# Experts of a two-layer MoE trunk in a fixed order, with the branch for overflowing rows ahead of them and a quarter of the value products moved

## The chip, the core and the metric

The kernel runs on one core of a Trainium2 chip. The core has a matrix engine (PE, with its weight loads shown apart as PEld), a vector engine (DVE), a scalar engine (ACT), GpSimd (POOL) and SyncE (SP), which here issues the DMAs that bring in the weights. The time is the device time of one execution in microseconds; of the kernel before there are three: 1061.95, 1063.36 and 1065.77, median 1063.36.

## What is computed

Two layers over 512 rows of 1024 values, all in float32. A layer has a token mixer beside a cross-attention to 256 fixed memory rows, an output projection and a layer norm, then a mixture of experts and another layer norm. This work concerns the mixture:

```
scores = sigmoid(x @ router_w);  a group of 4 experts of 16 is chosen, and 2 experts in it
gate   = their two scores, normalised;  combine[t, e] = gate of expert e for row t, else 0
for e in range(16):
    h   = silu(x @ w_gate[e]) * (x @ w_up[e])          # 1024 -> 512
    out = out + combine[:, e:e+1] * (h @ w_down[e])    # 512 -> 1024
```

The cross-attention of layer 1 needs `k, v = split(mem @ w_kv)`, which doesn't depend on the rows; the kernel computes it while layer 0's routing runs.

## The kernel before, in words

**Products.** A float32 product is three products of parts: each weight tile is copied to a high part on ACT (L168) and the rest, raw minus high, is made on DVE or GpSimd (L169); `mm3` (L202 to L204) multiplies high by high, low by high and high by low. Right-hand sides are split in the same way (`split_to`, L207 on ACT and L208 on DVE).

**Weights.** A class `Stream` (W) brings all weights in order, 1 MB a load, by SP (L147), into raw pages of 8 KB a partition. There are 24 pages, which the mixture's other tiles share too. `W.rings(8)` sets eight of them aside for split parts (ten after expert 5, which leaves nine for raw weights in layer 0 and eleven in layer 1). `flight` is how many loads may be under way (four in the mixture), `keep` how many pages stay free (four from expert 12 on). `W.pump()` issues splits and loads as long as there are pages, and is called at the end of each `W.done(g)`, when a split tile has been used. `W.on_pool(n)` says which splits go to GpSimd.

**An expert.** `gather(e)` (L667) fetches up to 128 rows by an indirect DMA of GpSimd; `xtrans(e)` transposes them (L676) and splits them to `xgt`; `gate_up(e)` makes 48 products into `ga` and `ua`, Silu on ACT (L692) and the multiplication on DVE (L693); `htrans(e)` transposes h (L699) and splits it to `ht`; `down(e)` makes 24 products into `ya` and two evictions on ACT with the gate as scale (L714); `scatter(e)` (L663) adds the rows to the result by an indirect DMA. The loop issues for each e: gate_up(e), xtrans(e+1), gather(e+3), down(e-1) and its scatter, htrans(e). An expert's weights are six loads: gate, up, gate, up in halves of the 1024 rows, then two of the down weights of the expert before.

**Overflow.** Rows beyond 128 of an expert are left to `more(i, ...)` (L887): every engine reads the number `nover` (L889) and branches (L890) around a loop that the data rarely enter. It is called in the loop at e == 0, and its page `rest` is dropped behind it. An engine that reads the number waits for DVE's last write, and its earlier work has to be done before it.

**Order.** The tile scheduler decides each engine's order by its own simulated times; a `tc.manual_schedule` makes it keep the order of the code on the engines named, and `tc.issue_after(x)` keeps an instruction behind x.

**Layer 0's head.** While the routing runs (tables made by `tab` products, L626), `fill0` calls `keys_values()`: keys (`ka`), then 48 value products (`va`) in four quarters (j), then two splits to `vt`. In it GpSimd takes some of the splits.

Of the kernel before, what the change touches and what calls it, by code (L numbers as in the profile page):

```python
# [23 lines left out]
OP = mybir.AluOpType  # L24
# [3 lines left out]
P = 128  # L28
# [19 lines left out]
def trunk(ctx, tc, x, mem, w_in_a, sgu_ln_g, sgu_ln_b, sgu_w, sgu_b, w_in_b, conv_w, w_kv, w_out,  # L48
# [15 lines left out]
    def page(name, shape, dtype=FT, of=None):  # L64
        of = free_pages if of is None else of
        assert of, f"no page for {name}; held: {sorted(v[1] for v in held.values())}"
        i = of.pop(0)
        uid[0] += 1
        t = pages.tile(shape, dtype, name=f"{name}_{uid[0]}", tag=f"pg{i}", bufs=1)
        held[id(t)] = (i, name, t)  # L70
        return t

    def drop(*ts):
        for t in ts:
            i, name, _ = held.pop(id(t))
            W.home(name).append(i)
# [123 lines left out]
    def mm3(o, a, b, start, stop):  # L200

        pe.matmul(o, a[0], b[0], start=start, stop=False)  # L202
        pe.matmul(o, a[0], b[1], start=False, stop=False)  # L203
        return pe.matmul(o, a[1], b[0], start=False, stop=stop)  # L204
# [111 lines left out]
    drop(memp)  # L316
    keep_warm(8)

    def keys_values():
        kt = page("kt", [P, 2, H, NMEM], FR)  # L320
        vt = page("vt", [P, 2, 2, MW], FR)
        a = [acc("ka") for _ in range(H)]
        for j in range(4):
            g = W.next()
            for kk in range(2):
                k = 2 * j + kk
                for h in range(H):
                    cs = slice(h * P, (h + 1) * P)
                    mm3(a[h][:, :NMEM], (g[:, 0, kk, cs], g[:, 1, kk, cs]), (memh[:, k, :], meml[:, k, :]),
                        k == 0, k == KB - 1)  # L330
            W.done(g)
        for h in range(H):
            split_to(kt[:, 0, h, :], kt[:, 1, h, :], a[h][:, :NMEM])
        a = [acc("va") for _ in range(2)]
        for j in range(4):
            g = W.next()
            for kk in range(2):
                k = 2 * j + kk
                for m in range(2):
                    ms = slice(m * P, (m + 1) * P)  # L340
                    mm3(a[m], (memh[:, k, ms], meml[:, k, ms]), (g[:, 0, kk, :], g[:, 1, kk, :]),
                        k == 0, k == KB - 1)
            W.done(g)
        for m in range(2):
            split_to(vt[:, 0, m, :], vt[:, 1, m, :], a[m])
        return kt, vt
# [303 lines left out]
    def experts(i, lnp, fill, after, stop, fine=False):  # L650
# [15 lines left out]
        def gather(e):  # L666
            pool_e.indirect_dma_start(out=xg[:, e % 2], out_offset=None, in_=x1d[i],  # L667
                                      in_offset=bass.IndirectOffsetOnAxis(ap=tabs[e][0], axis=0),
                                      bounds_check=S - 1, oob_is_err=False)
# [9 lines left out]
        def gate_up(e, between=None):  # L679
            a = [acc("ga"), acc("ua")]  # L680
            for half in range(2):
                if half and between is not None:
                    between()
                for u in range(2):
                    for j in range(2):
                        g = W.next()
                        for kk in range(2):
                            k = 4 * half + 2 * j + kk
                            m = mm3(a[u], (xt[:, 0, k, :], xt[:, 1, k, :]), (g[:, 0, kk, :], g[:, 1, kk, :]),
                                    k == 0, k == KB - 1)  # L690
                        W.done(g)
            act.activation(hp[:, 0, :], a[0], AF.Silu)  # L692
            vec.tensor_tensor(hp[:, 1, :], hp[:, 0, :], a[1], op=OP.mult)  # L693
            return m

        def htrans(e):
# [5 lines left out]
        def down(e, evict):  # L702
            for n in range(2):
                o = acc("ya")
                for j in range(2):
                    g = W.next()
                    for kk in range(2):
                        k = 2 * j + kk
                        mm3(o, (ht[:, 0, k, :], ht[:, 1, k, :]), (g[:, 0, kk, :], g[:, 1, kk, :]), k == 0, k == 3)
                    W.done(g)  # L710
                evict(n, o)

        def scaled(e):
            return lambda n, o: act.activation(ys[e % 2][:, n * 512:(n + 1) * 512], o, AF.Copy, scale=tabs[e][1])  # L714
# [4 lines left out]
            with tc.issue_after(last_entry[-1]):  # L719
                keep_warm(8)  # L720
        fill()
        rest = page("more", [P, 4, FE])
        W.keep, W.flight = 0, 4
        W.ahead, W.whole, W.on_pool = 6, True, lambda n: False
        W.rings(8)
        W.pump()
        xtrans(0)
        gather(2)
        for e in range(E):
            up = gate_up(e, (lambda: (down(last - 1, scaled(last - 1)), scatter(last - 1))) if e == last else None)  # L730
            if e + 1 < E:
                xtrans(e + 1)
            if e + 3 < E:
                gather(e + 3)
            if e == 0:
                more(i, rest)
                drop(rest)
                W.pump()
            if e == 5:
                W.parts += 2  # L740
            if 0 < e < last:
# [326 lines left out]
    W.keep = 3  # L1068

    def fill0():  # L1070
        kv1.append(keys_values())
        drop(memh, meml)
    xhl = []

# [79 lines left out]
```

## Time and profile before

| | |
|---|---|
| runs | 1061.95, 1063.36, 1065.77 us, median 1063.36 |
| profiled execution, its own time | 1063.26 us |
| its span, first to last instruction | 1061.6 us |
| mean granted clock of PE | 0.970 of 2.4 GHz |
| busy: PE, PEld, DVE, ACT, POOL | 991.3, 812.6, 780.7, 628.6, 170.8 us |
| HBM read, written | 262.22, 26.21 MB |

The span is 1.7 us shorter than the execution's own time, and all rows below are on its clock. Layer 0's experts lie at 215 to 535 us, layer 1's at 730 to 1040. Products are pipelined: a row's length is its latency, and two in a row start closer than that, so the pace is read from starts.

### The profile page before, as it was taken

To read this page: it belongs to the slowest core of one execution; us is meant where nothing else is said; L and a number is where in the kernel's file an instruction comes from. 1 tells how busy PE (TensorE), PEld (TensorE's weight loads), DVE (VectorE), ACT (ScalarE), POOL (GpSimd) and SP (SyncE) were. 2 spreads that over 40 slices of the span, in tenths; PEclk is the share of its full clock that TensorE was granted. 3 is DMA by queue.
4 is the path that set the end of the run, shared out by engine and by line. 5 is a ranking of instruction groups with operands and counts; after the bars stand their busy time and mean duration, and the time that the engine had idled before them with its cause. 6 is when DMAs were issued, how large, how long until landed. Compare 5 with 4: busy or idle time off the path is not lost. (4 is left out here: it accounts for less than half of the span.)

```text
span 1061.6 us, 12769 instructions
## 1 busy us (share of the span) xinstructions
PE 991.3 (93%) x4815; PEld 812.6 (77%) x4816; DVE 780.7 (74%) x880; ACT 628.6 (59%) x682; POOL 170.8 (16%) x115
## 2 busy tenths in 40 slices
PE   8999999769999999899899999986699999998995
PEld 6788889658888887678679887875588888886873
DVE  4638667866889976788794656475789999777885
ACT  4526533446788865767653514232688888767762
POOL 0000004311222212101101000212022222221123
PEclk9999999979999999999999999986899999999998
DMA  9713358568999999999690414492499999999934
GB/s 323 274 41 119 120 198 296 181 224 287 361 371 307 396 350 330 319 319 338 175 390 26 159 51 159 148 390 74 172 362 349 371 341 376 354 356 335 333 67 157
DMA packets 102220, 273.31 MB, mean 257 GB/s; under 512 B 10442, under 2 KB 10966, under 8 KB 102152
## 3 DMA queue, kind: packets, MB, share of 16 engines
q1 hardware_dynamic: 89480, 242.84, 62.8%
q0 software_dynamic: 11808, 26.97, 9.1%
q10 hardware_dynamic: 864, 2.62, 0.7%
q8 instruction: 39, 0.64, 0.2%
q14 instruction: 29, 0.24, 0.1%
HBM read 262.22 MB, written 26.21 MB: 272 GB/s over the span
## 5 line engine op out<-in xcount | busy, mean ns | idle before, releaser
L169 DVE TENSOR_TENSOR low<-raw,high 128x2048 fp32r<-128x2048 f32 x189 | 429.8, 2290 | 90.6 <-ACT high L168 87.2
L168 ACT ACTIVATE high<-raw 128x2048 fp32r<-128x2048 f32 x189 | 358.2, 1913 | 44.8 <-PE ga L204 33.4
L168 ACT ACTIVATE split<-raw 128x1024 fp32r<-128x1024 f32 x66 | 68.5, 1058 | 76.5 <-PE za L204 26.0
L203 PE MATMUL ua<-low,xgt 128*128 128x512 f32 x248 | 97.8, 394 | 9.0 <-DVE low L169 9.0
L202 PE MATMUL ya<-high,ht 128*128 128x512 f32 x256 | 103.5, 406 | 1.3 <-ACT high L168 1.3
L203 PE MATMUL ya<-low,ht 128*128 128x512 f32 x256 | 102.3, 400 | 2.1 <-DVE low L169 2.1
L204 PE MATMUL ya<-high,ht 128*128 128x512 f32 x256 | 101.8, 398 | 0.8 <-DVE ht L208 0.7
L203 PE MATMUL ga<-low,xgt 128*128 128x512 f32 x248 | 99.9, 403 | 2.1 <-DVE low L169 1.9
L202 PE MATMUL ga<-high,xgt 128*128 128x512 f32 x248 | 100.4, 405 | 0.0
L204 PE MATMUL ga<-high,xgt 128*128 128x512 f32 x248 | 98.1, 396 | 0.0
L169 DVE TENSOR_TENSOR split<-raw,split 128x1024 fp32r<-128x1024 f32 x57 | 68.7, 1221 | 39.7 <-ACT split L168 38.9
L202 PE MATMUL ua<-high,xgt 128*128 128x512 f32 x248 | 97.4, 393 | 0.1
L204 PE MATMUL ua<-high,xgt 128*128 128x512 f32 x248 | 96.9, 391 | 0.0
L667 POOL DMA_INDIRECT xg<-x1d,idxs x32 | 49.8, 1556 | 267.6 <-PE xt L676 238.3
L169 POOL TENSOR_TENSOR split<-raw,split 128x1024 fp32r<-128x1024 f32 x9 | 21.7, 2406 | 284.8 <-DVE sto L474 148.9
L207 ACT ACTIVATE xgt<-xt 128x512 fp32r<-128x512 f32 x64 | 36.4, 592 | 50.3 <-PE ua L203 26.0
L202 PE MATMUL za<-xh,split 128*128 128x512 f32 x160 | 61.9, 393 | 2.0 <-ACT xh L207 2.0
L203 PEld LDWEIGHTS ua<-low,xgt 128*128 128x128 f32 x248 | 46.6, 188 | 21.0 <-DVE low L169 11.7
L203 PE MATMUL za<-xl,split 128*128 128x512 f32 x160 | 62.5, 391 | 0.0
L204 PE MATMUL za<-xh,split 128*128 128x512 f32 x160 | 61.5, 390 | 0.0
L203 PEld LDWEIGHTS ya<-low,ht 128*128 128x128 f32 x256 | 48.6, 190 | 13.7 <-DVE low L169 3.1
L202 PEld LDWEIGHTS ya<-high,ht 128*128 128x128 f32 x256 | 48.6, 190 | 12.9 <-ACT high L168 1.8
(250 smaller groups left out, 1899.1 us busy)
## 6 DMA issues: line engine op xcount, KB each, us to landing
raw<-in_w_gate_dram SPq DMA_DIRECT2D x64, 1024.0 KB, 8.8
raw<-in_w_up_dram SPq DMA_DIRECT2D x64, 1024.0 KB, 8.3
raw<-in_w_down_dram SPq DMA_DIRECT2D x64, 1024.0 KB, 9.5
raw<-in_w_kv_dram SPq DMA_DIRECT2D x8, 1024.0 KB, 7.0
raw<-in_w_out_dram SPq DMA_DIRECT2D x8, 1024.0 KB, 6.1
raw<-in_w_in_b_dram SPq DMA_DIRECT2D x8, 1024.0 KB, 10.2
raw<-in_w_in_a_dram SPq DMA_DIRECT2D x6, 1024.0 KB, 5.5
x1d<-x POOLq DMA_DIRECT2D x8, 512.0 KB, 5.8
```

The source lines that it names most:

```text
L168: act.activation(high, src, AF.Copy)
L169: (pool_e if self.on_pool(self.count) else vec).tensor_tensor(low, src, high, op=OP.subtract)
L202: pe.matmul(o, a[0], b[0], start=start, stop=False)
L203: pe.matmul(o, a[0], b[1], start=False, stop=False)
L204: return pe.matmul(o, a[1], b[0], start=False, stop=stop)
L207: r = act.activation(hi, src, AF.Copy)
L667: pool_e.indirect_dma_start(out=xg[:, e % 2], out_offset=None, in_=x1d[i], in_offset=bass.IndirectOffsetOnAxis(ap=tabs[e][0], axis=0), bou ...
```

## The change

1. Experts 0 to 14 are issued under `tc.manual_schedule` for PE, ACT and DVE; it is closed at e == 15, so the last expert is left to the scheduler.
2. `more` moves ahead of the loop, behind `fill()` and ahead of xtrans(0); its scratch is the page of h, and the page `rest` is gone. `W.pump()` stands behind xtrans(0) and gather(2).
3. In `gate_up` Silu is issued right behind gate's last product, and the multiplication ahead of the last `W.done`; in `down` the eviction stands ahead of `W.done`, so each is ahead of the splits which that call issues.
4. In layer 0 the value products of j == 3 are issued behind the last product of the tables, and GpSimd takes no split of `fill0`.

```diff
-    def keys_values():
+    def keys_values(after=None):
...
+                    with ExitStack() if after is None or j < 3 else tc.issue_after(after):
+                        mm3(a[m], (memh[:, k, ms], meml[:, k, ms]), (g[:, 0, kk, :], g[:, 1, kk, :]),
+                            k == 0, k == KB - 1)
...
+                        if half and u and j:
+                            vec.tensor_tensor(hp[:, 1, :], hp[:, 0, :], a[1], op=OP.mult)
                         W.done(g)
-            act.activation(hp[:, 0, :], a[0], AF.Silu)
-            vec.tensor_tensor(hp[:, 1, :], hp[:, 0, :], a[1], op=OP.mult)
+                    if half and not u:
+                        act.activation(hp[:, 0, :], a[0], AF.Silu)
...
+                    if j:
+                        evict(n, o)
                     W.done(g)
-                evict(n, o)
...
         fill()
-        rest = page("more", [P, 4, FE])
+        more(i, hy)
         W.keep, W.flight = 0, 4
         W.ahead, W.whole, W.on_pool = 6, True, lambda n: False
         W.rings(8)
-        W.pump()
         xtrans(0)
         gather(2)
+        W.pump()
+        order = ExitStack()
+        order.enter_context(tc.manual_schedule(engines={ET.PE, ET.Activation, ET.DVE}))
         for e in range(E):
+            if e == last:
+                order.close()
...
-            if e == 0:
-                more(i, rest)
-                drop(rest)
-                W.pump()
...
     def fill0():
-        kv1.append(keys_values())
+        W.on_pool = lambda n: False
+        kv1.append(keys_values(last_entry[-1]))
```

What it does to the engines' orders shows at three places; line numbers of the changed kernel are up to five higher.

ACT in layer 0, around Silu and the two evictions of the same late expert (number 10). Before:

```order
L207 ACTIVATE ht<-htr 128x512
L168 ACTIVATE high_3431<-raw_3216 128x2048
L168 ACTIVATE high_3462<-raw_3234 128x2048
L207 ACTIVATE xgt_1693<-xt 128x512
L692 ACTIVATE h_1692<-ga 128x512
L168 ACTIVATE high_3480<-raw_3272 128x2048
L207 ACTIVATE xgt_1693<-xt 128x512
L168 ACTIVATE high_3498<-raw_3292 128x2048
L714 ACTIVATE y_170<-ya,gates 128x512
L168 ACTIVATE high_3516<-raw_3323 128x2048
L207 ACTIVATE ht<-htr 128x512
L714 ACTIVATE y_170<-ya,gates 128x512
```

Now:

```order
L168 ACTIVATE high_3481<-raw_3274 128x2048
L168 ACTIVATE high_3499<-raw_3294 128x2048
L696 ACTIVATE h_1692<-ga 128x512
L168 ACTIVATE high_3519<-raw_3324 128x2048
L207 ACTIVATE xgt_1693<-xt 128x512 x2
L718 ACTIVATE y_170<-ya,gates 128x512
L168 ACTIVATE high_3556<-raw_3342 128x2048
L718 ACTIVATE y_170<-ya,gates 128x512
L168 ACTIVATE high_3576<-raw_3360 128x2048
L207 ACTIVATE ht<-htr 128x512
L168 ACTIVATE high_3606<-raw_3380 128x2048
L168 ACTIVATE high_3624<-raw_3417 128x2048
```

Two more high parts stand ahead of Silu, one more ahead of the first eviction; both xgt copies are together behind Silu's split, and between the evictions there is one split and no longer the copy of ht.

DVE in layer 0, from the last selectors of the tables (`sel`) to the branch. Before:

```order
L617 TENSOR_SCALAR sel<-slot_91,pos_99 128x128 x2
L169 TENSOR_TENSOR split_1868<-raw_1225,split_1868 128x1024
L208 TENSOR_TENSOR vt_1701<-va,vt_1701 128x512
L633 TENSOR_SCALAR idxs<-tab 128x16
L634 TENSOR_REDUCE gates<-tab 128x16
L604 TENSOR_TENSOR ovf<-cnt,thr 1x48
L607 TENSOR_REDUCE ovn<-ovf 1x1
L608 CAST flags<-ovf 1x48
L609 CAST nover<-ovn 1x1
L169 TENSOR_TENSOR low_1931<-raw_1310,high_1930 128x2048
L208 TENSOR_TENSOR vt_1701<-va,vt_1701 128x512
L169 TENSOR_TENSOR low_1894<-raw_1254,high_1893 128x2048
```

Now:

```order
L618 TENSOR_SCALAR sel<-slot_91,pos_99 128x128 x2
L634 TENSOR_SCALAR idxs<-tab 128x16
L635 TENSOR_REDUCE gates<-tab 128x16
L169 TENSOR_TENSOR low_2081<-raw_1310,high_2080 128x2048
L169 TENSOR_TENSOR low_2057<-raw_1254,high_2056 128x2048
L208 TENSOR_TENSOR vt_1701<-va,vt_1701 128x512
L605 TENSOR_TENSOR ovf<-cnt,thr 1x48
L208 TENSOR_TENSOR vt_1701<-va,vt_1701 128x512
L608 TENSOR_REDUCE ovn<-ovf 1x1
L609 CAST flags<-ovf 1x48
L610 CAST nover<-ovn 1x1
L893 TENSOR_LOAD nover
```

The number `nover` was followed by the splits, with the branch further back, behind expert 0's last subtraction; now both low parts and both `vt` stand between the tables and the branch, and the branch stands directly behind the number.

PE in layer 0, the last value products (`va`), the products of the tables (`tab`) and the count (`cnt`). Before:

```order
L202 MATMUL va<-split_1811,memh_128 128x512
L203 MATMUL va<-split_1811,memh_128 128x512
L204 MATMUL va<-split_1811,meml_129 128x512
L626 MATMUL tab<-tok,sel 128x48 x2
L602 LDWEIGHTS ones_b
L602 MATMUL cnt<-oh,ones_b 128x16
L602 LDWEIGHTS ones_b
L602 MATMUL cnt<-oh,ones_b 128x16
L602 LDWEIGHTS ones_b
L602 MATMUL cnt<-oh,ones_b 128x16
L602 LDWEIGHTS ones_b
L602 MATMUL cnt<-oh,ones_b 128x16
```

Now:

```order
L627 MATMUL tab<-tok,sel 128x48 x3
L204 MATMUL va<-split_1784,meml_129 128x512
L202 MATMUL va<-split_1784,memh_128 128x512
L203 MATMUL va<-split_1784,memh_128 128x512
L204 MATMUL va<-split_1784,meml_129 128x512
L627 MATMUL tab<-tok,sel 128x48 x5
L202 MATMUL va<-split_1811,memh_128 128x512
L203 MATMUL va<-split_1811,memh_128 128x512
L204 MATMUL va<-split_1811,meml_129 128x512
L202 MATMUL va<-split_1811,memh_128 128x512
```

The last two products of the tables stood behind the last value product; now all of them are done when the last quarter of the value products (on split_1811) begins.

## Rows read from the trace of the kernel before

**Rows 1.** The page: busy us of each engine over the whole span, its share and its number of instructions; and the group of DVE's subtractions for half a load, with their number, busy us and mean ns.

```profile
PE 991.3 (93%) x4815; PEld 812.6 (77%) x4816; DVE 780.7 (74%) x880; ACT 628.6 (59%) x682; POOL 170.8 (16%) x115
...
L169 DVE TENSOR_TENSOR split<-raw,split 128x1024 fp32r<-128x1024 f32 x57 | 68.7, 1221 | 39.7 <-ACT split L168 38.9
```

**Rows 2.** Table of 20 us windows: stretch, its length, then for PE, PEld, DVE, ACT and POOL the busy us and the number of instructions, PE's granted clock, DMA share, GB/s. The first lies early, the second and third late in layer 0's loop, the last in layer 1's.

```profile
260.00:280.00 20.00, 20.00 (x95) 16.55 (x94) 17.56 (x12) 15.96 (x15) 5.95 (x3) 1.00 0.98 348
...
420.00:440.00 20.00, 18.08 (x83) 14.37 (x83) 13.77 (x9) 13.87 (x12) 2.62 (x2) 1.00 0.91 299
...
460.00:480.00 20.00, 17.95 (x82) 14.06 (x81) 15.48 (x10) 15.47 (x13) 1.57 (x1) 1.00 0.96 321
...
860.00:880.00 20.00, 20.00 (x94) 16.55 (x93) 18.63 (x12) 16.06 (x16) 6.19 (x3) 1.00 1.03 395
```

**Rows 3.** Timeline of PE, the four transposes of h of one expert each (start us, us, engine, line, operation): experts 1, 2, 5 and 14 of layer 0, expert 14 of layer 1.

```profile
258.12 0.60 PE L699 MATMUL htr<-ident,h 128*128 128x128 f32 x4
...
276.08 0.60 PE L699 MATMUL htr<-ident,h 128*128 128x128 f32 x4
...
330.01 0.60 PE L699 MATMUL htr<-ident,h 128*128 128x128 f32 x4
...
501.56 0.60 PE L699 MATMUL htr<-ident,h 128*128 128x128 f32 x4
...
1009.56 0.60 PE L699 MATMUL htr<-ident,h 128*128 128x128 f32 x4
```

**Rows 4.** What PE waited for from 400 to 545 us (layer 0's late experts): total us, times, longest us.

```profile
PE ua L203 <- DVE low L169: 5.1, 3, 1.8
...
PE ga L203 <- DVE low L169: 1.0, 2, 0.5
```

**Rows 5.** Timeline of ACT in expert 10 of layer 0; in brackets the idle time ahead and what ended it.

```profile
420.85 0.69 ACT L714 ACTIVATE y<-ya,gates 128x512 f32<-128x512 f32 x1 [4.29 <-PE ya L204]
...
421.43 1.90 ACT L168 ACTIVATE high<-raw 128x2048 fp32r<-128x2048 f32 x1
```

**Rows 6.** Groups of instructions from 260 to 380 us: line, engine, operation, tiles, shapes, number | busy us, mean ns | idle before.

```profile
L169 DVE TENSOR_TENSOR low<-raw,high 128x2048 fp32r<-128x2048 f32 x41 | 93.4, 2291 | 10.9 <-ACT high L168 9.5 <-DMA raw<-in_w_gate_dram 0.8 <-DMA raw<-in_w_down_dram 0.5
...
L168 ACT ACTIVATE high<-raw 128x2048 fp32r<-128x2048 f32 x41 | 78.2, 1915 | 12.4 <-PE ga L204 8.6 <-PE ua L204 3.7
...
L208 DVE TENSOR_TENSOR xgt<-xt,xgt 128x512 fp32r<-128x512 f32 x13 | 8.4, 684 | 0.3 <-ACT xgt L207 0.3
...
L714 ACT ACTIVATE y<-ya,gates 128x512 f32<-128x512 f32 x6 | 4.1, 690 | 2.5 <-PE ya L204 2.5
```

**Rows 7.** Timeline of all engines in the head of layer 0's experts (start us, us, engine, line, operation).

```profile
183.58 2.41 POOL L169 TENSOR_TENSOR split<-raw,split 128x1024 fp32r<-128x1024 f32 x1
...
183.62 2.45 DVE L559 TENSOR_TENSOR route<-route,rb 128x48 f32<-128x48 f32 x1 [0.31 <-ACT route L556]
...
204.47 0.48 DVE L617 TENSOR_SCALAR sel<-slot,pos 128x128 fp32r<-128x128 f32 x2
...
208.94 0.30 PE L626 MATMUL tab<-tok,sel 128*128 128x48 f32 x2
...
210.20 1.09 POOL L667 DMA_INDIRECT xg<-x1d,idxs  x1 [1.15 <-DVE gates L634]
...
214.19 1.95 PE L676 MATMUL xt<-ident,xg 128*128 128x128 f32 x8 [3.87 <-DMA xg<-x1d,idxs]
...
215.33 0.60 ACT L207 ACTIVATE xgt<-xt 128x512 fp32r<-128x512 f32 x1 [2.14 <-PE xt L676]
...
219.41 0.77 PE L202 MATMUL ga<-split,xgt 128*128 128x512 f32 x1
...
226.29 0.39 PE L202 MATMUL ga<-high,xgt 128*128 128x512 f32 x1
...
229.01 0.39 PE L202 MATMUL ua<-high,xgt 128*128 128x512 f32 x1
...
237.08 0.68 DVE L208 TENSOR_TENSOR xgt<-xt,xgt 128x512 fp32r<-128x512 f32 x1
...
237.97 1.09 PE L699 MATMUL htr<-ident,h 128*128 128x128 f32 x4 [5.59 <-DVEq L890]
```

**Rows 8.** The same in the head of layer 1's experts.

```profile
729.51 0.14 DVE L609 CAST nover<-ovn 1x1 int32<-1x1 f32 x1
...
730.90 2.81 PE L676 MATMUL xt<-ident,xg 128*128 128x128 f32 x12 [1.96 <-DMA xg<-x1d,idxs]
...
754.41 1.09 PE L699 MATMUL htr<-ident,h 128*128 128x128 f32 x4 [7.14 <-DVEq L890]
```

**Rows 9.** What SP's queue waited for from 340 to 400 us: total us, times, longest us. A wait for `DMA raw` is one for an older load to land, one for `DVE low` one for a page.

```profile
SPq L147 <- DMA raw<-in_w_down_dram: 17.2, 6, 3.3
...
SPq L147 <- DMA raw<-in_w_gate_dram: 11.2, 5, 3.3
...
SPq L147 <- DMA raw<-in_w_up_dram: 9.8, 6, 2.5
```

**Rows 10.** Line 147, which issues the weight loads, from 340 to 400 us: SP's one wait for each load with its count, the first and last start; the last row is the time from issue to landing.

```profile
L147 SPq EVENT_SEMAPHORE  x18: 17/17/17, 342.1 to 398.0; - x18
...
DMA to landing us min/median/max: 11.4/12.3/12.7
```

**Rows 11.** The same wait of line 147 from 260 to 300 us.

```profile
L147 SPq EVENT_SEMAPHORE  x14: 17/17/28, 260.8 to 299.5; - x14
```

More of the change, by code (lines that the diff above doesn't have):

```diff
@@ L340, in keys_values @@
                     ms = slice(m * P, (m + 1) * P)
-                    mm3(a[m], (memh[:, k, ms], meml[:, k, ms]), (g[:, 0, kk, :], g[:, 1, kk, :]),
-                        k == 0, k == KB - 1)
+                    with ExitStack() if after is None or j < 3 else tc.issue_after(after):
+                        mm3(a[m], (memh[:, k, ms], meml[:, k, ms]), (g[:, 0, kk, :], g[:, 1, kk, :]),
+                            k == 0, k == KB - 1)
             W.done(g)
```

## The prediction

> **What bounds the kernel now.** I read the busy times first: PE is busy 93% of the span and no other engine over 74% [rows 1]. So only what leaves PE idle, or at half clock, can be won. The table of 20 us windows shows where that is [rows 2]: from 260 us on PE works 20.00 of 20 us with some 95 instructions in a window, and between 420 and 480 us, in the same loop of layer 0, only about 18 with 82 or 83. The transposes of h (one group per expert) give the pace: from 276.08 to 330.01 us three experts pass, 17.98 us each; from 258.12 to 501.56 us thirteen, 18.73 each [rows 3]. So 17.98 us is an expert bound by PE, and layer 0 loses 243.4 - 13 x 17.98 = 9.7 us after its first expert.
>
> What PE waits for in those stretches is split weights, above all those that DVE's subtraction ends (5.1 us before ua) [rows 4]. ACT shows why they are late: it stands 4.29 us before an eviction of y and only then makes the next high part [rows 5]. The splits are behind the evictions in ACT's order, though ACT's and DVE's work for one expert has room: six high parts of 1.915 us are 11.5, and two xgt, one ht, one Silu (near 0.6 each) and two evictions (0.69) make it 15.3 us; six low parts of 2.291 and four smaller operations of 0.68 are 16.5 us on DVE [rows 6, 7]. Both are under 17.98.
>
> The other loss is the branch for the overflowing rows, which today stands behind expert 0. In layer 0 PE waits 5.59 us for DVE to reach it, and in layer 1 7.14 us [rows 7, 8].
>
> **The change part by part.**
>
> *Layer 0's head, value products and splits.* Today the last two products of the tables stand at 208.94 us behind all 48 value products, though their last selector was done at 204.47 + 0.48 = 204.95 [rows 7]. Ahead of the last 12 value products they can run near 205.8, so the first gather, today at 210.20, can start near 206.7. The four subtractions that leave GpSimd (2.4 us each) become four of 1.22 us on DVE [rows 1], 4.9 us; but beside the first of them a small routing operation on DVE took 2.45 us, as long as GpSimd's split itself, 2.41 [rows 7], which then need not be. With some 2 us back at two such places I count the two as equal. The 12 value products left end at 205.8 + 0.3 + 12 x 0.227 = 208.8 us.
>
> *The branch ahead of expert 0, layer 0.* Every engine now passes it before the first transposes, and PE's wait moves there. DVE has (second order listing) two low parts, two vt and four small operations ahead of the branch, and both low parts write pages that the last value product reads: 208.8 + 2 x 2.29 + 2 x 0.69 + 0.7 = 215.5 us. The gather has landed by then: today its data let xt start 4.0 us after its start [rows 7], so near 210.7. xt(0) starts at 215.7; today ga follows xt(0)'s first transpose 5.2 us later because xt(1) stands between, whereas now it needs only the copy on ACT, which ends 1.14 + 0.60 us after that transpose: 217.5 against 219.41 [rows 7]. The 48 products of expert 0 take 10.9 us at 0.227 each (twelve between 226.29 and 229.01), and 1.4 more for a slow start as today (24 products between 219.41 and 226.29): 229.8. The mult, one low part and the xgt subtraction (0.68 + 2.29 + 0.68) stand on DVE before the second expert's third product, at 233.5, so its products effectively begin at 233.0. From there to its htr is one period less its own 0.6 us: 250.4, against 258.12 in [rows 3]. **Gain at expert 1: 7.7 us.** SP, too, drains at the branch; its expert loads are then issued, and the next one waits for a page in any case, so I cost this at nothing. An extra load of ACT's function table falls into the wait for the gather or for DVE.
>
> *The same in layer 1.* The branch's number is ready at 729.51 + 0.14 us, with no splits ahead of it now, and xt(0) waits for the gather until 730.90 as today. Eight transposes instead of twelve put ga near 732.6 [rows 8]; 48 products and 0.5 us of slow start end at 744.0. Of expert 0's weights half is split before the branch; the other low parts follow at 2.29 us from 734.9, when the first product tile frees a page: 737.2, 739.5, 741.8, 744.1, each 1.5 to 3 us ahead of use. Then the same three operations: products of expert 1 effectively from 747.3, its htr at 764.7.
>
> *The fixed order.* In it no split stands behind an eviction that PE has not nearly reached (first order listing); Silu and mult come at once. Thirteen periods of 17.98 are 233.7 us: htr of expert 14 at 250.4 + 233.7 = 484.1 in layer 0 (today 501.56) and 998.4 in layer 1 (today 1009.56) [rows 3]. **Leads of 17.5 and 11.2 us, 28.7 together.** Expert 15, free to be reordered, and the tail I carry over at their present lengths.
>
> *What I take off.* The order fixes the margins too: following the operations through one expert, three low parts of six come only 0.7 to 0.9 us before their product. I allow 0.1 us an expert, 2.6. And the stream of weights: SP spent 38 of the 60 us from 340 to 400 waiting for loads in flight [rows 9], and issued 18 loads from 342.1 to 398.0, 3.29 us each [rows 10], where PE at 17.98 us an expert eats one per 3.00. With nine pages for raw weights in layer 0 after expert 5 and 12 us until a load lands, the lead is 9 x 3.00 - 12 = 15 us; over the 54 loads left it shrinks by 54 x 0.29 = 15.7, 0.7 us too much. In layer 1 two pages more cover it. With 1.3 us for the last loads, for which fewer pages are kept, that is 2.0.
>
> **Sum:** 28.7 - 2.6 - 2.0 = 24.1 us off the profiled execution's own 1063.26, which stands 0.1 from the median of 1063.36: **1039 us.**
>
> Bounds: the fixed order's margin may cost nothing (1036.6), or 0.5 us an expert, the longest wait of ga today [rows 4] (1046); the head of layer 0 may gain nothing (7.7 us less: 1047), or be better by the 1.4 us of its slow start. For expert 15, whose new order I have no row for, I leave 4 us either way.
>
> A rule on branches: behind today's branch PE starts 0.2 us after DVE's last operation before it (237.08 + 0.68 against 237.97 [rows 7]), so I charge nothing for the jump itself. Were there a fetch from memory in it, the nearest row is the gather's 4.0 us until its data are used, 8 us for two branches: 1047. The Trainium skill, Runtime: NRT & Kernel Launch, section Instruction fetch mechanics, says that a taken branch to a target outside the window fetched ahead stalls for a fetch. No such gap shows in the row.
>
> **Rivals.**
>
> *A: the loads become the bound.* If the 3.29 us per load of [rows 10] hold from the first expert on, an expert takes 19.7 us, 1.76 more, 24.6 us in 14 experts of a layer, less the lead of 15 and (two more pages) 21: 9.6 + 3.6 = 13 us lost, 1063.3 - 28.7 + 13 + 2.6 = 1050; without the lead of layer 1's two pages and with landings later still I let it reach 1058. For it: a DMA share of 0.98 and 1.03 in the full windows [rows 2]. Against it: from 260.8 to 299.5 us SP issued 14 loads, 2.98 us each [rows 11]. The Trainium skill, SBUF — State Buffer, section Summary: rules for kernel authors, would have about 358 GB/s for transfers between HBM and SBUF; an expert's 6.29 MB of weights and 1.05 MB of rows would then take 20.5 us, 2.5 more, and the sum would be 1072, slower than before. The window from 860 to 880 us moved 395 GB/s [rows 2], so I don't take it as a ceiling.
>
> *B: slower.* ACT and DVE are now chained in one order, each high part behind xgt, ht or an eviction that waits for PE, and PE behind the low part. If the loop runs in lockstep and each expert meets one wait like today's longest for ua (1.8 us [rows 4]), 26 experts lose 47 us where 28.7 were won: 1081. It decides at 28.7 / 26 = 1.1 us an expert, a period of 19.1. For it: the margin under 1 us, and that today's late experts show such waits. Against it: in those the order, not the amount of work, was late, and DVE held PE at 20.00 with 18.63 of 20 us busy [rows 2].
>
> *C: no change.* The scheduler's own order goes back to the same waits elsewhere (expert 15, or loads after the loop): 1061 to 1065.
>
> **How the numbers follow.** My forecast (1029 to 1049) 0.65, A (1049 to 1058) 0.17, B 0.11, C 0.07. Three microseconds, 0.3%, are about what a measurement of this kernel can tell from no change. Faster: forecast, and A, 0.82; same: C, 0.07; slower: B, 0.11. The range leaves out B, most of C and what lies below the better bound: 1029 to 1058.
>
> **What would show it.** Right: no wait for the branch behind expert 0, a wait of about 6 us ahead of xt(0) in layer 0 and none beyond the gather's in layer 1; htr of expert 1 near 250 us; PE at 20.00 in the windows from 400 to 480, periods near 18.0 to 18.2 up to expert 14. Wrong: periods over 19 with SP waiting for landings (A) or PE for low parts with loads long landed (B); or a first gather still near 210 us.

## The result and the profile after

The changed kernel takes 1032.24 us (median of four runs, 1029.19 to 1035.55); the kernel before, run beside it, 1064.57. The ratio is 0.9692 (0.9644 to 0.9739). The forecast was 1039 in a range of 1029 to 1058. Its profiled execution took 1031.97 us, with a span of 1030.1 where before had 1061.6.

The page after, busy us of each engine and DVE's subtractions for half a load:

```profile
PE 983.7 (95%) x4815; PEld 810.6 (79%) x4816; DVE 774.2 (75%) x884; ACT 627.7 (61%) x684; POOL 200.5 (19%) x111
...
L169 DVE TENSOR_TENSOR split<-raw,split 128x1024 fp32r<-128x1024 f32 x61 | 73.6, 1221 | 39.6 <-ACT split L168 38.9
```

PE does the same 4815 instructions, and four more half splits are DVE's (57 in [rows 1]). Where the time came from is read from marks that both executions have. Windows after, columns as in [rows 2], three of layer 0's loop:

```profile
260.00:280.00 20.00, 20.00 (x97) 16.68 (x96) 17.88 (x12) 15.83 (x13) 5.69 (x2) 1.00 1.02 364
420.00:440.00 20.00, 20.00 (x94) 16.57 (x94) 17.88 (x12) 16.21 (x14) 5.69 (x2) 1.00 1.02 358
460.00:480.00 20.00, 20.00 (x94) 16.55 (x93) 17.87 (x12) 14.72 (x13) 2.49 (x1) 1.00 0.99 354
```

The second and third windows stood at 18.08 and 17.95 us with some 82 products [rows 2]; now PE never stops. The transposes of h of expert e are called htr(e) below, the first transposes of its gathered rows xt(e). After: htr of experts 1, 14 and 15 of layer 0, the first product of layer 0's final stage, then htr of experts 1 and 14 of layer 1:

```profile
250.22 0.60 PE L702 MATMUL htr<-ident,h 128*128 128x128 f32 x4
...
483.05 0.60 PE L702 MATMUL htr<-ident,h 128*128 128x128 f32 x4
...
502.18 0.60 PE L702 MATMUL htr<-ident,h 128*128 128x128 f32 x4
...
509.68 0.70 PE L785 MATMUL ra<-x,ident 128*128 128x512 f32 x1
...
747.15 0.60 PE L702 MATMUL htr<-ident,h 128*128 128x128 f32 x4
...
980.20 0.60 PE L702 MATMUL htr<-ident,h 128*128 128x128 f32 x4
```

The marks of before that [rows 3] lack: expert 15 and the final stage of layer 0, expert 1 of layer 1:

```profile
526.62 0.66 PE L699 MATMUL htr<-ident,h 128*128 128x128 f32 x4 [0.96 <-DVE h L693]
...
534.67 0.59 PE L781 MATMUL ra<-x,ident 128*128 128x512 f32 x1
...
778.68 0.60 PE L699 MATMUL htr<-ident,h 128*128 128x128 f32 x4
```

Thirteen experts of layer 0 now take 483.05 - 250.22 = 232.83 us, 17.91 each. All stretches, in us (the last product of a layer's output projection starts at 175.10 and 703.60 in before, at 173.24 and 678.73 after; the last of the final stage in layer 1 at 1048.87 and 1017.42):

| stretch | before | after | gained | forecast |
|---|---|---|---|---|
| up to layer 0's projection | 175.10 | 173.24 | 1.9 | 0 |
| on to htr(1), layer 0 | 83.02 | 76.98 | 6.0 | 7.7 |
| htr(1) to htr(14) | 243.44 | 232.83 | 10.6 | 9.7 |
| htr(14) to the final stage | 33.11 | 26.63 | 6.5 | 0 |
| on to layer 1's projection | 168.93 | 169.05 | -0.1 | 0 |
| on to htr(14), layer 1 | 305.96 | 301.47 | 4.5 | 11.2 |
| on to the last product | 39.31 | 37.22 | 2.1 | 0 |

That is 31.5 us of the 31.5 by which the spans differ; the forecast's 28.7 had 4.6 taken off for margins and loads. The first 1.9 us belong to no part of the change: a second execution of the changed kernel reached the same product at 174.83, and one of the kernel before with the fixed order alone at 173.41.

The head of layer 0 after, all engines:

```profile
202.62 0.48 PE L627 MATMUL tab<-tok,sel 128*128 128x48 f32 x2 [1.01 <-DVE sel L618]
...
204.17 1.08 POOL L668 DMA_INDIRECT xg<-x1d,idxs  x1 [22.48 <-DVE gates L635]
...
205.80 4.50 DVE L169 TENSOR_TENSOR low<-raw,high 128x2048 fp32r<-128x2048 f32 x2 [2.38 <-ACT high L168]
...
211.73 0.14 DVE L610 CAST nover<-ovn 1x1 int32<-1x1 f32 x1
...
213.43 1.95 PE L677 MATMUL xt<-ident,xg 128*128 128x128 f32 x8 [7.40 <-DVEq L894]
...
231.59 0.79 PE L204 MATMUL ga<-high,xgt 128*128 128x512 f32 x1 [1.71 <-DVE xgt L208]
```

Tables and gather moved 6 us forward, 1.9 of them since the projection was earlier, but xt(0) did not: it waits 7.40 us for the branch, since DVE writes the branch's number at 211.73 + 0.14, behind two low parts. Against [rows 7] the 5.59 us of wait at htr are gone, and 7.40 us stand at xt, where the gather's 3.87 stood. The head of layer 1 after, the same columns:

```profile
704.48 0.13 DVE L610 CAST nover<-ovn 1x1 int32<-1x1 f32 x1
...
706.02 1.95 PE L677 MATMUL xt<-ident,xg 128*128 128x128 f32 x8 [2.12 <-PEq L894]
...
712.60 1.92 ACT L168 ACTIVATE high<-raw 128x2048 fp32r<-128x2048 f32 x1 [3.99 <-DVE low L169]
...
714.60 2.29 DVE L169 TENSOR_TENSOR low<-raw,high 128x2048 fp32r<-128x2048 f32 x1 [2.09 <-ACT high L168]
...
716.93 3.72 ACT L168 ACTIVATE high<-raw 128x2048 fp32r<-128x2048 f32 x2 [2.42 <-DVE low L169]
...
718.88 4.68 DVE L169 TENSOR_TENSOR low<-raw,high 128x2048 fp32r<-128x2048 f32 x2 [1.98 <-ACT high L168]
...
723.47 0.68 DVE L693 TENSOR_TENSOR h<-h,ua 128x512 f32<-128x512 f32 x1
...
724.21 1.11 PE L702 MATMUL htr<-ident,h 128*128 128x128 f32 x4 [3.51 <-DVE h L693]
```

ACT and DVE go by turns here: high 712.60, low 714.60, high 716.93, low 718.88, each waiting for the other, 4.3 us a link. By the code, no page is free for a high part, so each takes the raw page that the low part before it releases (tested below with more pages). The mult, behind the last low part, ends at 724.15, and PE waits 3.51 us. Then TensorE's clock is down. Two windows after, one behind PE's wait of 1.71 us in layer 0, one behind this one:

```profile
233.00:238.00 5.00, 5.00 (x19) 3.98 (x18) 2.30 (x2) 1.92 (x1) 0.00 (x0) 0.82 0.83 319
...
727.00:734.00 7.00, 6.67 (x17) 5.26 (x18) 3.72 (x5) 2.67 (x2) 0.00 (x0) 0.56 0.85 288
```

SP's queue from 400 to 480 us after; what it waited for, and line 147 as in [rows 10]:

```profile
SPq L147 <- DMA raw<-in_w_up_dram: 23.6, 8, 4.7
SPq L147 <- DMA raw<-in_w_gate_dram: 22.6, 8, 4.6
SPq L147 <- DMA raw<-in_w_down_dram: 20.9, 8, 3.5
```

```profile
L147 SPq EVENT_SEMAPHORE  x24: 17/17/17, 401.9 to 477.7; - x24
```

67 of 80 us wait for landings, and the 24 loads come (477.7 - 401.9) / 23 = 3.30 us apart. PE uses one in 17.91 / 6 = 2.99. The loads are slower than PE here, and yet PE waits for none. From 340 to 400 us they still came 2.98 us apart (20 loads).

### The profile page after: what moved, and what is told of

The parts are those of the page before. It is cut to its first block, busy times and chain, and to the rows that moved or that the text cites. A ratio compares the mean times of both kernels' runs of the same rounds, so it can differ in the third digit from the quotient of the medians.

```text
span 1030.1 us, 12721 instructions
## 1 busy us (share of the span) xinstructions
PE 983.7 (95%) x4815; PEld 810.6 (79%) x4816; DVE 774.2 (75%) x884; ACT 627.7 (61%) x684; POOL 200.5 (19%) x111
## 5 line engine op out<-in xcount | busy, mean ns | idle before, releaser
L668 POOL DMA_INDIRECT xg<-x1d,idxs x32 | 83.2, 2601 | 299.6 <-PE xt L677 270.5
L169 DVE TENSOR_TENSOR split<-raw,split 128x1024 fp32r<-128x1024 f32 x61 | 73.6, 1221 | 39.6 <-ACT split L168 38.9
L169 POOL TENSOR_TENSOR split<-raw,split 128x1024 fp32r<-128x1024 f32 x5 | 11.9, 2383 | 267.0 <-DVE sto L475 147.0
L204 PEld LDWEIGHTS ga<-high,xgt 128*128 128x128 f32 x248 | 47.4, 191 | 14.1 <-DVE xgt L208 4.0
L204 PEld LDWEIGHTS ya<-high,ht 128*128 128x128 f32 x256 | 48.1, 188 | 12.8 <-DVE ht L208 1.3
L664 POOL DMA_INDIRECT rd<-h,idxs x16 | 40.4, 2523 | 89.3 <-ACT h L718 79.6
L202 PEld LDWEIGHTS ya<-high,ht 128*128 128x128 f32 x256 | 48.4, 189 | 10.5 <-ACT ht L207 0.6
```

What stands on the lines that cost most here:

```text
L169: (pool_e if self.on_pool(self.count) else vec).tensor_tensor(low, src, high, op=OP.subtract)
L664: added[e] = pool_e.indirect_dma_start(out=rd[i], out_offset=bass.IndirectOffsetOnAxis(ap=tabs[e][0], axis=0), in_=ys[e % 2], in_offset=No ...
```

## Experiments

Medians in us; each ratio is to the kernel before on the same chip (1063.8 to 1064.31).

**The order taken away.** Everything else of the change stays, the scheduler orders the experts.

```diff
-        order.enter_context(tc.manual_schedule(engines={ET.PE, ET.Activation, ET.DVE}))
```

> The changed kernel with the order of all experts left to the scheduler again (no manual schedule); the early branch, the moved Silu, mult and evictions and the head stay. My theory: the 10.7 us that layer 0's loop gained between the h transposes of experts 1 and 14, the 4.5 us of layer 1 and the 8.4 us that expert 15 gained in the two layers all come from splits that the fixed order keeps ahead of PE; without it waits of PE for DVE's low parts return in the late experts, expert 15 is back at some 25 and 22 us, and the time is 1048 to 1058. Rival: the moved Silu, mult and evictions, and loads that start earlier, carry the loop without the fixed order: 1038 or less, periods below 18.2.

Measured: 1048.33 (1045.44 to 1049.93), 0.9851 (0.9816 to 0.9886). PE's waits from 250 to 520 us:

```profile
PE ua L203 <- DVE low L169: 5.4, 4, 1.8
PE ga L203 <- DVE low L169: 1.4, 3, 0.5
PE ya L202 <- ACT high L168: 1.3, 1, 1.3
```

Waits of the size of [rows 4] are back, and expert 15 is back at 25.07 us after expert 14 (19.13 with the order). So the order up to expert 14 also shortens the one that is not in it.

**The order alone**, on the kernel before, with the branch, the head and the Silu of before.

```diff
+        order = ExitStack()
+        order.enter_context(tc.manual_schedule(engines={ET.PE, ET.Activation, ET.DVE}))
         for e in range(E):
+            if e == last:
+                order.close()
```

> The kernel before with the fixed order for experts 0 to 14 alone; branch behind expert 0, Silu, mult, evictions and layer 0's head as before. My theory: the order alone keeps the splits ahead, so the loops run at 17.9 us an expert from expert 1 on and expert 15 has no waits; only the heads lose against the change: 1040 to 1046. Rival: the order alone is worth what its loss took from the changed kernel, 12 to 16 us: 1048 to 1052.

Measured: 1037.56 (1036.32 to 1038.24), 0.9749 (0.9722 to 0.9775), below what theory and rival gave. PE waits for nothing from 255 to 505 us. At the branch it waits, first from 205 to 260 us, then from 705 to 760:

```profile
PE htr L699 <- DVEq L894: 2.6, 1, 2.6
...
PE htr L699 <- DVEq L894: 9.2, 1, 9.2
```

From layer 0's projection to the last product this takes 849.5 us, before 873.8 and the changed kernel 844.2: the order alone is 24.3 of 29.6 us, more than I gave it. The parts do not add up: the other three without the order (the experiment above, 857.0) are worth 16.8 us, on top of it 5.3. Those 5.3 lie almost all in layer 1's head (htr(1) 73.25 us behind the projection, against 68.42). In layer 0 htr(1) stands at 76.96 us behind the projection, as in the changed kernel (76.98), though branch and head are those of before: in the order one low part less stands ahead of the branch on DVE, which is through 57.2 us behind the projection, before 62.7, and the wait there is 2.6 us, not 5.59.

**The branch back behind expert 0.**

```diff
-        more(i, hy)
+        rest = page("more", [P, 4, FE])
...
+            if e == 0:
+                more(i, rest)
+                drop(rest)
+                W.pump()
```

> The changed kernel with the branch for overflowing rows back in the loop behind expert 0 and its own scratch page, the fixed order kept. My theory: PE waits 5 to 9 us for DVE behind expert 0 in each layer and runs slowly after it; the h transposes of expert 1 come some 7 us later in layer 0 and 4 to 6 us later in layer 1, nothing of it is made up, since the loop is bound by PE: 1042 to 1048. Rival: the loop catches up, since loads lie ready, or the splits done before the branch pay for it: 1036 or less.

Measured: 1037.4 (1036.46 to 1040.05), 0.9745 (0.9713 to 0.9777), between theory and rival. PE's waits, the first from 205 to 260 us, the second from 700 to 770:

```profile
PE htr L702 <- DVEq L898: 3.5, 1, 3.5
...
PE htr L702 <- DVEq L898: 9.9, 1, 9.9
```

In layer 1 the early branch is worth 6.7 us (htr(1) 75.16 us behind the projection against 68.42). In layer 0 it is worth nothing: xt(0) starts 5.0 us earlier with the branch behind it, yet htr(1) stands at 76.27 us behind the projection, against 76.98 and 75.33 in two executions of the changed kernel. Three more executions with the same head (further below) had 74.85, 77.84 and 77.94, so differences under 3 us at this mark say nothing; xt(0) stood at 40.17 to 40.20 in all five.

**Layer 0's head as before.**

```diff
-        W.on_pool = lambda n: False
-        kv1.append(keys_values(last_entry[-1]))
+        kv1.append(keys_values())
```

> The changed kernel with layer 0's head as before: value products free of the tables, GpSimd splitting there as before. My theory from the trace after: the first transposes of layer 0 wait 7.4 us for DVE to pass the branch, and the gather has landed 4 to 5 us before, so tables and gather that come 3 to 4 us later change nothing; DVE gets there at the same time or up to 2 us sooner without the four splits: 1030 to 1034. Rival, my prediction's step: tables 3 us earlier are worth their 3 us: 1035 to 1037.

Measured: 1036.88 (1034.44 to 1037.69), 0.9745 (0.9717 to 0.9772). The timeline of all engines:

```profile
210.15 1.08 POOL L668 DMA_INDIRECT xg<-x1d,idxs  x1 [2.91 <-DVE gates L635]
...
213.71 0.14 DVE L610 CAST nover<-ovn 1x1 int32<-1x1 f32 x1
...
215.88 1.52 PE L677 MATMUL xt<-ident,xg 128*128 128x128 f32 x6 [5.61 <-DMA xg<-x1d,idxs]
```

The gather is back at 210.15, xt(0) waits for its data instead of the branch, and xt(0) comes 42.64 us behind the projection instead of 40.19. My theory, that the branch hides the earlier tables, falls: both DVE's number and the gather had become earlier.

**Expert 15 in the order too**: `order.close()` behind the loop.

> The changed kernel with expert 15 in the fixed order too (closed behind the loop). Its h transposes now come 19.1 and 19.6 us behind expert 14's, 1.2 and 1.7 us over a period of 17.92. My theory: the scheduler's freedom there is worth nothing, the order of the code gives the same within 2 us a layer: 1029 to 1036. Rival: the freedom is what gave expert 15 its 6 and 2 us, and with the selector work and the loads of rows in order PE waits there: 1037 to 1042.

Measured: 1043.67 (1038.94 to 1044.37), 0.98 (0.9772 to 0.9828). PE's waits from 482 to 517 us, then from 985 to 1012:

```profile
PE selt L757 <- DVE selt L754: 4.8, 1, 4.8
...
PE selt L757 <- DVE selt L754: 2.6, 1, 2.6
```

That is some 12 us more than the changed kernel; the two waits are 7.4 us of it, in one of the faster executions (1039.73). The theory falls, the rival holds, if by more than it gave. The last expert's selectors stand on DVE behind splits that PE does not need yet (they start at 504.30; in an execution of the changed kernel at 485.24); a free order lets them by.

**Two fewer pages for raw weights** from expert 5 on: `W.parts += 4` in place of 2.

> The changed kernel with four instead of two pages taken from the raw weights after expert 5, so seven in layer 0 and nine in layer 1 are left for loads. After the change a load in layer 0 lands as late as 1.6 us before its split, in layer 1 about 10 us. My theory: the loop of layer 0 is PE-bound by a hair; two pages are 6 us of lead, so PE begins to wait for loads and loses 4 to 6 us in the last experts of layer 0 and nothing in layer 1: 1036 to 1040. Rival: the lead is set by the landing time and by how fast SP may issue, not by pages; the time stays at 1032.

Measured: 1032.7 (1030.52 to 1033.65), 0.969 (0.9654 to 0.9726). ACT's waits from 400 to 510 us:

```profile
ACT high L168 <- DMA raw<-in_w_down_dram: 6.3, 6, 3.2
ACT high L168 <- DMA raw<-in_w_gate_dram: 5.8, 4, 2.6
```

In the changed kernel ACT has no such wait there. The lead is used up, as the theory of the loads says, but PE waits only 0.2 us and the time does not move, as the rival says. The loads end the loop with hardly a page in hand; a loop a little longer, or two pages fewer again, should be held by them (not tried).

**The branch left out.** This kernel leaves out the rows beyond 128 of an expert.

```diff
-        more(i, hy)
```

> The changed kernel without the branch and the code for overflowing rows behind it (rows beyond 128 of an expert are left out). After the change the first transposes start 1.6 us (layer 0) and 1.4 us (layer 1) behind DVE's last operation ahead of the branch. My theory: that is the branch itself, reading the number and jumping on all engines; in layer 0 the two low parts still stand ahead on DVE, so 2 to 4 us are gained there, in layer 1 the gather lands at about the same time and little is gained: 1027 to 1030. Rival, my prediction: the jump costs nothing: 1031 to 1033.

Measured: 1026.14 (1024.41 to 1028.32), 0.9642 (0.9605 to 0.9679). In layer 0 xt(0) starts at 208.19, 2.1 us after PE asks for the gathered rows, 34.93 us behind the projection instead of 40.19, and htr(1) at 70.52 instead of 75.33 to 76.98; in layer 1 htr(1) gains 0.4 to 0.9. So the branch still costs some 5 us where two low parts stand ahead of its number, and under one where none does.

**The two low parts of layer 0 behind the split of xt(0)**, so that the number is written ahead of them.

```diff
-            (pool_e if self.on_pool(self.count) else vec).tensor_tensor(low, src, high, op=OP.subtract)
+            with ExitStack() if self.after_low is None else tc.issue_after(self.after_low):
+                (pool_e if self.on_pool(self.count) else vec).tensor_tensor(low, src, high, op=OP.subtract)
...
-        xtrans(0)
+        first = xtrans(0).ins
+        W.after_low = None if i else first
```

> The changed kernel with the two low parts of layer 0's head put behind expert 0's xgt subtraction on DVE, so that the branch's number is made right behind the tables and the value products. My theory: the first transposes start 4 us sooner, when the gather has landed, and everything behind them with them: 1027 to 1029. Rival: the loads, only 1.6 us ahead at the worst place, are now the bound in layer 0, or expert 0 waits for the later low parts: 1031 to 1033.

Measured: 1028.54 (1027.0 to 1030.37), 0.9662 (0.9634 to 0.969). The timeline:

```profile
209.23 0.14 DVE L611 CAST nover<-ovn 1x1 int32<-1x1 f32 x1
...
210.93 1.75 PE L678 MATMUL xt<-ident,xg 128*128 128x128 f32 x8 [3.12 <-DVEq L899]
```

xt(0) stands 35.87 us behind the projection, against 40.2 in the changed kernel and 34.93 without the branch; htr(1) at 70.77, almost as without the branch (70.52). So the low parts are most of the wait, the branch's own jump the smaller part. Layer 0's loop still takes 232.83 us, so the loads do not take the gain back. By the times alone it would not be clear: the ratio's interval overlaps that of the changed kernel run again (0.9669 to 0.9718).

**More free pages in layer 1's head.** First three more, in `mixer_end`:

```diff
-                W.keep, W.ahead = (2, 3) if i == 0 else (1, 2)
+                W.keep, W.ahead = (2, 3) if i == 0 else (4, 2)
```

> The changed kernel with three pages more kept free in layer 1's head, so three loads fewer lie ready and the split parts have pages at once. After the change the first three splits of layer 1's loop stand in a chain (each high part waits for the low part before it, whose raw page it takes), the mult comes 3.5 us late and PE runs slowly after it. My theory: with free pages the wait of the h transposes for the mult (3.5 us), that of ga for xgt (1.2) and about 2 us of slow products go: 1025 to 1028. Rival: the mult is late by the order on ACT and DVE, not by pages, or fewer loads ready cost as much: 1031 to 1033.

Measured: 1031.04 (1028.37 to 1035.74), 0.9675 (0.9646 to 0.9705). PE's first wait from 700 to 760 us, then two rows of the timeline:

```profile
PE xt L677 <- DMA xg<-x1d,idxs: 7.5, 1, 7.5
```

```profile
704.95 2.46 POOL L668 DMA_INDIRECT xg<-x1d,idxs  x1 [15.04 <-DVE gates L635]
...
706.53 0.37 SPq L147 DMA_DIRECT2D raw<-in_w_gate_dram  x1
```

The wait of htr for the mult is gone, so the missing pages were its cause. But a load of 1 MB is now under way beside the gather, and xt(0) waits 7.5 us for its rows, elsewhere about 2: one wait for another. The rows landed 8.4 us after the gather's start, in the same place elsewhere 4.2 to 4.5. Not all of it need be the load's: the gather itself took 2.46 us on GpSimd, beside a subtraction of DVE, in place of 1.08. No run parts the two.

**One more page, and the low parts behind xt(0)**: the edit in `split()` above, and

```diff
-                W.keep, W.ahead = (2, 3) if i == 0 else (1, 2)
+                W.keep, W.ahead = (2, 3) if i == 0 else (2, 2)
```

> The changed kernel with two edits at once: the two low parts of layer 0's head behind expert 0's xgt subtraction, and one page more kept free in layer 1's head, so that the first split of layer 1's loop is whole before the branch and no load of 1 MB is issued beside the gather (with three pages one was, and the gather's data came 7.5 us late). My theory: layer 0's part repeats its 6 us, and in layer 1 the chain of high and low parts is one link shorter: the h transposes of expert 1 come 1 to 3 us sooner after layer 1's projection; 1025 to 1028. Rival: layer 1's mult stays late, since the chain only moves: 1028 to 1030.

Measured: 1023.42 (1021.6 to 1025.12), 0.962 (0.9596 to 0.9644), faster than both kernels. PE's waits from 690 to 750 us:

```profile
PE xt L678 <- DMA xg<-x1d,idxs: 2.5, 1, 2.5
```

Neither the wait for the mult nor the 7.5 us is there, and htr(1) of layer 1 stands 62.51 us behind the projection, where the changed kernel has 68.42 and 67.94, a gain of 5.4 to 5.9 us where 1 to 3 were expected. The prediction had 764.7 - 703.6 = 61.1.

**Silu and mult as before, the order kept**: both stand behind the last product of `ua` again, and the evictions of y at their old place.

> The changed kernel with Silu, the multiplication and the evictions issued where they were, behind the splits, the fixed order and the rest kept. My theory: one low part more (2.3 us) stands ahead of the multiplication on DVE, but PE has 24 products of the expert before to do until it needs h, so the loop stays at 17.9 us an expert; only expert 0, which has none, waits some 2 us more in each layer: 1033 to 1037. Rival B of my prediction in this form: the margins of under 1 us break, each expert meets a wait of 0.5 us or more: 1045 and above.

Measured: 1029.45 (1029.05 to 1031.28), 0.9679 (0.9653 to 0.9706). PE's wait in layer 1's head:

```profile
PE htr L700 <- DVE h L694: 5.7, 1, 5.7
```

PE waits for nothing from 251 to 500 us and the loop takes 233.28 us. The theory's 2 us a layer do not show in the time, and B is out. So the early Silu and mult carry nothing that can be measured here.

**The changed kernel again**, beside the last three.

> The changed kernel itself once more, for comparison on the same chip: 1030 to 1034 us, the h transposes 17.9 us apart in both loops.

Measured: 1031.4 (1029.38 to 1035.38), 0.9694 (0.9669 to 0.9718). The interval of the best kernel lies below this one. In this execution the wait for xgt behind htr(0) was 1.71 us again, but the clock behind it stayed up:

```profile
234.60:239.60 5.00, 5.00 (x24) 4.14 (x23) 3.79 (x2) 3.15 (x2) 0.00 (x0) 1.00 0.93 316
```

From htr(0) to htr(1) it took 20.27 us where the first execution took 21.80, and htr(1) stood 75.33 us behind the projection.

## Why the prediction was right, and where it was not

**The loop (forecast 9.7 in layer 0, measured 10.6).** Right, and shown: without the order the waits return, with the order alone they are gone. The period is 17.91 us, where 17.98 was taken.

**Charges of 4.6 us.** Not paid. The low parts come in time in every expert: PE waits for nothing from 251 to 500 us. The pace of the loads was read rightly, 3.30 us each against the 3.29 of [rows 10], and the lead of pages paid for it. Rival A's step that failed is that this pace holds from the first expert on: from 340 to 400 us the loads came 2.98 us apart, only from 400 on 3.30, and over 24 loads that takes 24 x 0.31 = 7.5 us of lead, less than its 15. Two pages fewer show how near it was. The Trainium skill, SBUF — State Buffer, section Summary: rules for kernel authors, gives about 358 GB/s for transfers between HBM and SBUF. The trace after agrees with it over a long stretch, 355 GB/s from htr(1) to htr(14) in layer 0; the one window of 395 in [rows 2] was a poor reason to set it aside. What made that price too high, 1072, was the 1.05 MB of rows an expert: the indirect DMAs moved 6.9 MB over these 13 experts, 0.53 each. With that the page's figure gives 6.82 MB / 358 GB/s = 19.1 us an expert, an estimate, 1.1 over the period, or 16 us in 14 experts, about the lead.

**Expert 15 and layer 0's end (forecast 0, measured 6.5 and 2.1).** This step failed: I carried it over because it is not in the order. 3.0 us are waits of before from 500 to 536 us, which return without the order; one of 1.0 for h stands in the row at 526.62, the others are:

```profile
PE ya L202 <- ACT high L168: 1.3, 1, 1.3
...
PE ya L204 <- DVE ht L208: 0.7, 1, 0.7
```

Another 2.7 us are twelve products of y that stood behind htr(14) and now stand ahead of it, so that they belong to the loop. Together, from htr(1) to the final stage, 17.1 us were gained; PE's waits there were 11.2 in before and none after. The rest is what a wait costs beyond its row, which counts from the end of the product before: from start to start, PE's gaps over 0.3 us hold 20.2 us beyond the 0.227 of a product in before and 3.2 after, a difference of 17.0. A part of that the clock took (0.89 from 418 to 428 us in before, 1.00 after).

**Head of layer 0 (forecast 7.7, measured 6.0).** The times came as forecast, from the same projection: tables and gather early, the wait at DVE's number (xt(0) forecast 40.6 us behind the projection, measured 40.19), third product of expert 1 forecast at 233.5, 231.6 with the experts' start 1.9 us earlier, measured 231.59. The missing 1.7 us are the clock's: behind that wait of 1.71 us it was 0.82 from 233 to 238 us, with products 0.43 us apart instead of 0.23. In the second execution it stayed at 1.00, and the gain was 83.02 - 75.33 = 7.7 us, the forecast's own; in all five with this head it was 5.1 to 8.2. But the step that gave this gain to the early branch and the earlier tables failed: it took the 5.59 us at the branch for a cost that stays unless the branch moves. With the order alone, branch and tables as before, htr(1) comes as early (76.96), and that wait is 2.6. In layer 0 the branch's move put one wait in place of another; that the forecast of htr(1) was met is in this part luck.

**Head of layer 1 (forecast 11.2 for htr(14), measured 4.5).** The step that failed: "the other low parts follow at 2.29 us". I let only DVE set the pace and did not ask where the high parts find a page. They follow at 4.3 us, PE waits 3.51 us, and the clock behind it (0.56 from 727 to 734 us) and a wait of 1.16 for xgt cost 5.0 us more up to htr(1). The runs with more pages show it: the wait goes.

**The jump charged at nothing.** In layer 0, 213.43 - 211.87 = 1.56 us pass from the number to PE's first instruction, in layer 1 706.02 - 704.61 = 1.41. The row I had used, 0.2 us, was one in which PE had read the number and branched 9 us before. In layer 0 after, what PE's sequencer did with the number (duration in ns, start in us):

```profile
L893 PEldq TENSOR_LOAD <-nover x1: 487/487/487, 211.9 to 211.9; - x1
...
L894 PEldq COMPARE_BRANCH  x1: 353/353/353, 212.5 to 212.5; - x1
```

The reading starts at once, the branch ends at 212.86, the next instruction starts 0.06 us behind it, and four waits for semaphores fill the time to 213.40. The Trainium skill, Runtime: NRT & Kernel Launch, section Instruction fetch mechanics, says that a taken branch whose target lies outside the window fetched ahead stalls for a fetch. The trace shows no such stall behind the branch; one inside its 0.35 us it cannot show. What counts for the time is less than 1.56 us: without the branch xt(0) of layer 0 starts 35.87 - 34.93 = 0.9 us sooner than with the low parts behind it.

**Rivals.** B is out: there is no lockstep in the loop, not even with Silu and mult at their old place. Its chain was seen in one place, layer 1's head, for want of pages. C is out: the ratio's interval ends at 0.9739, and no such waits came back.

**Why the sum was near all the same.** Layer 1's head gave 6.7 us less than forecast and layer 0's 1.7 less, expert 15 8.6 more, the charges 4.6 and the loop 0.9 more; 1.9 came from an execution that started its experts earlier. The mechanism of the loop was right; that the 8.4 us missed in the heads and the 8.6 won at expert 15 cancel is luck.

## What to carry to other kernels

Where the engine that bounds a loop waits for operands that other engines have time to make, look at what those engines do first: an order with the splits ahead of the evictions was worth 24 us here by itself, the changed kernel's PE doing the same 4815 instructions, and the piece left to the scheduler gained as well. Run each part of a change alone too: three parts worth 16.8 us without that order were worth 5.3 with it. Where a branch is moved, follow what stands ahead of its number on the engine that writes it; here two subtractions ahead of it cost 4.3 us at the first transposes and the branch itself 0.9. And follow a chain of two engines through the pages: a link that must wait for its page runs at the sum of both operations, and behind every wait of the bounding engine ask what its clock may take.

## What the runs showed of the hardware

- Weight loads of 1 MB came 3.30 us apart over 24 loads while their queue waited for landings 67 of 80 us; over 233 us the kernel moved 355 GB/s.
- Where a 1 MB load started 1.6 us after a gather of up to 128 rows, the rows landed 8.4 us after the gather's start, against 4.2 to 4.5 in the other kernels; 1.4 us of it lie in the gather's own instruction, 2.46 us beside a subtraction of DVE.
- A number just written was read by each engine in 0.46 to 0.55 us in layer 0 and 0.29 to 0.32 in layer 1, and PE branched on it in 0.35 and 0.32; PE's first product behind the branch started 1.4 to 1.6 us after the number. In the kernel before, where PE had branched 9 us earlier, it started 0.2 us after DVE's last operation ahead of its own.
- PE's waits of 1.7 and 3.5 us were followed by stretches with a granted clock of 0.82 and 0.56, partly at the lower level; these cost 1.7 and 3.8 us, as much as the waits. After the same wait of 1.7 us in another execution of the same kernel the clock stayed at 1.00; of the five executions with layer 0's head of the changed kernel, all with this wait, it fell behind it in three.
- Two executions of the same kernel reached layer 0's experts 1.6 us apart, which is as much as a part of this change may be worth: single executions were compared from a mark of their own.
